# Softmax attention on one core: queries and keys of twelve pairs of heads transposed by TensorE and VectorE instead of by DMA, with other numbers in the planner

## The chip, the core and the metric

The kernel runs on one core of a Trainium2 chip. The metric is the device time of one execution in microseconds (us), as the median of several runs. A core has five engines that run side by side, each working through its own instructions in order: TensorE (PE, with its weight loads as PEld), VectorE (DVE), ScalarE (ACT), GpSimd (POOL) and SyncE (SP). SP does no arithmetic; here it issues nearly all DMA transfers. Transfers of all queues are carried out by the same 16 DMA engines.

## The reference

Attention over 8 batches and 8 heads, 512 positions, 64 dimensions, in float32:

```python
scale = 1.0 / np.sqrt(q.shape[-1])
scores = np.einsum('bhqd,bhkd->bhqk', q, k) * scale
scores = scores - scores.max(axis=-1, keepdims=True)
attn = np.exp(scores)
attn = attn / attn.sum(axis=-1, keepdims=True)
return np.einsum('bhqk,bhkd->bhqd', attn, v).astype(np.float32)
```

q, k and v are drawn from the standard normal distribution. The kernel takes no maximum off the scores.

## The kernel before

**Tiles.** The 64 heads are worked through as 32 pairs, g = 0 to 31. A pair's q, k and v are each one load of 128 partitions x 512 elements (256 KB). POOL casts them to float16: k and q into `qkp` (L343), v into one of 12 tiles `vp` (L335) that have a column of ones behind the 64 columns of v. For the scores, q and k have to stand with their dimension on the partitions, so `qkp` is transposed into `tqk`: partitions 0 to 63 hold the first head, 64 to 127 the second.

**Scores and exps.** A pair has 8 score blocks (c, h): chunk c of 128 keys of head h against all 512 queries. Two blocks make a group m, 128 groups of two in all but for the last two blocks, which stand alone. A group is two matmuls on TensorE (L396) into a PSUM tile `st` (128 x 1024 float32, 3 buffers), then one exp on ScalarE (L401) into a float16 tile `pt`. The exps of the first three groups are started by hand in `first_pair`. A few groups are "raised" instead: VectorE computes the exp with a polynomial, in one instruction that reads PSUM (`raise_`, L415) and six passes on SBUF (`pass_`, L428, L439 and four at L450).

**Values.** A unit is 128 queries of a head: four matmuls with 65 columns (L484), which add up the four chunks of `pt` against `vp`; the column of ones gives the softmax's sum. Seven units share a PSUM tile `o`, and VectorE normalises them together: a reciprocal (L462) and a multiply (L463) into a ring of results, from which SP stores each finished head (L471, 128 KB). The last head is computed chunk by chunk (`last_values`, L499 to L519).

**Transposes.** There are two ways. On TensorE: eight 128x128 transposes per pair (L370, `transposes`, in two halves of four, k first) into a PSUM tile `tp`, and one VectorE copy to `tqk` (L377, `copy`). The tiles `tp` and `o` take turns in two PSUM banks, `x0` and `x1`. By DMA: one DMA transpose per pair that SP issues (L353, `transpose_by_dma`) from `qkp` to `tqk`. The pairs listed in `Plan.BY_DMA` (6, 8, ... 28) go the second way, all others but pair 0 the first. Pair 0 has its own path.

**What sets the order.** Instructions are issued in a written order (`manual_schedule`). The class `Plan` computes it before the kernel is built: it steps through time, 5 ns at a time, with a fixed cost for each kind of work (`TRANSPOSE` 225 ns a half, `V_UNIT` 130, `SLOT` 216 for a score group, `COPY` 615, `PASSES` 690 to 1335 and so on), and decides at each point what TensorE (`step_pe`) and VectorE (`step_dve`) do next. TensorE takes the next score group if a PSUM tile and the transposed operands will be there, else a half transpose, else a unit of values. VectorE takes a raise first, then copies and normalisations as they become ready. It starts a polynomial pass only if the pass, its time multiplied by `MARGIN`, ends early enough for what is ready or soon will be (`LATE_NORM`, `LATE_COPY`). `for_dve` says which groups are raised: only while at most `AHEAD` passes are pending and not in the last `LAST_PAIRS` pairs. A raised exp counts as ready `SLACK` ns after its last pass. For pairs in `BY_DMA` the plan holds the operands to be there at time 0.

**The feed.** With every fourth group (`feed(g)`, at the first scores of pair g) the DMA transpose of pair g+2, the loads of pair g+5, the casts of q and k of pair g+3 and that of v of pair g+2 are issued. Loads have 6 buffers of each kind, `qkp` has 3, `tqk` has 5. SP works in order, so a load or store stands behind a DMA transpose that waits for its casts. Pairs in `HALVED` (only pair 20) have v loaded in two halves.

Of the kernel before, what the change touches and what calls it, by code (L numbers as in the profile page):

```python
# [9 lines left out]
FP16 = mybir.dt.float16  # L10
# [6 lines left out]
class Plan:  # L17
# [22 lines left out]
    STEP = 5  # L40
    FIRST_UNIT = 4

    BY_DMA = (6, 8, 10, 12, 14, 16, 18, 20, 22, 24, 26, 28)
    LATE_NORM, LATE_COPY, HURRY, SOON, BACKLOG = 600, 800, 1400, 220, 1600
    LAST_PAIRS, AHEAD, MARGIN, SLACK, MOST = 2, 1, 1.05, 800, 7

    def __init__(self, groups, pairs, first):
        self.groups, self.pairs = groups, pairs
# [4 lines left out]
        for m in range(first):  # L53
            self.act += self.EXP + self.EXP_FIXED
            self.exps[m] = self.act + self.EXP_DONE
            self.read.append(self.exps[m])
        self.tq = {0: 5800, **{g: 0 for g in self.BY_DMA}}
        self.next_t = 1
# [118 lines left out]
    def step_pe(self, t):  # L177
        if self.m == len(self.groups):
            self.values(t)
            return  # L180
        while self.part_t == 0 and self.next_t in self.BY_DMA:
            self.next_t += 1
# [62 lines left out]
def kernel(  # L245
# [7 lines left out]
    nc = tc.nc  # L253
    B, H, S, D = q.shape
    P = 128
# [18 lines left out]
    cpool = ctx.enter_context(tc.tile_pool(name="const", bufs=1))  # L274
    lpool = ctx.enter_context(tc.tile_pool(name="load", bufs=6))
    qpool = ctx.enter_context(tc.tile_pool(name="qk16", bufs=3))
    tpool = ctx.enter_context(tc.tile_pool(name="tqk", bufs=5))
    ppool = ctx.enter_context(tc.tile_pool(name="pt", bufs=30))
    dpool = ctx.enter_context(tc.tile_pool(name="pd", bufs=3))
    wpool = ctx.enter_context(tc.tile_pool(name="work", bufs=1))  # L280
# [3 lines left out]

    NV = 12

    HALVED = range(20, 21)
    NU = 56
    ring = cpool.tile([P, NU, D], FP32, name="ring")
    vps = [cpool.tile([P, 2, NI, D + 1], FP16, name=f"vp{n}") for n in range(NV)]  # L290
# [4 lines left out]
    qkp = {}  # L295
    tqk = {}
# [12 lines left out]
    def load_tile(g, name):  # L309
        t = lpool.tile(  # L310
            [P, 2, NI, D],
            FP32,
            tag=f"{name}32",
            name=f"{name}32_{g}",
            bufs=6,
        )
        raw.setdefault(g, {})[name] = t
        return t

    def load(g, names):  # L320
        if g >= NP:
            return
        for name in names:
            src = {"q": q, "k": k, "v": v}[name]
            t = load_tile(g, name)
            if name == "v" and g in HALVED:
                for h in range(2):
                    nc.sync.dma_start(out=t[:, h], in_=source(src, g)[:, h])
                continue
            nc.sync.dma_start(out=t[:, :, :, :], in_=source(src, g))  # L330

    def cast_v(g):
        if g >= NP:
            return
        nc.gpsimd.tensor_copy(out=vps[g % NV][:, :, :, 0:D], in_=raw[g]["v"][:, :, :, :])  # L335

    def cast_qk(g):
        if g >= NP:
            return
        t = qpool.tile([P, 2, NI, P], FP16, tag="qkp", name=f"qkp_{g}")  # L340
        for n, name in ((1, "k"), (0, "q")):
            eng = nc.vector if (g, name) == (1, "q") else nc.gpsimd
            eng.tensor_copy(  # L343
                out=t[:, n].rearrange("p i (h d) -> p h i d", h=2),
                in_=raw[g][name][:, :, :, :],
            )
        qkp[g] = t

    def transpose_by_dma(g):
        if g not in Plan.BY_DMA:  # L350
            return
        tqk[g] = tpool.tile([P, 2, S], FP16, tag="tqk", name=f"tqk_{g}")
        nc.sync.dma_start_transpose(  # L353
            out=tqk[g].rearrange("p n (i c) -> p (n i) c", c=P),
            in_=qkp[g].rearrange("p n i c -> p (n i c)"),
        )

    def feed(g):
        transpose_by_dma(g + 2)
        load(g + 5, "kqv")  # L360
        cast_qk(g + 3)
        cast_v(g + 2)
# [260 lines left out]
    with tc.manual_schedule():  # L623
        first_loads()
        load(1, "kq")
        load(0, "v")
        for g in range(2, 5):
            load(g, "kq")
            load(g - 1, "v")
        load(4, "v")  # L630
        make_identity(nc, ident)
        for n in range(NV):
            nc.vector.memset(vps[n][:, :, :, D : D + 1], 1.0)
        first_pair()
        cast_qk(1)
        cast_v(0)
        cast_qk(2)
        cast_v(1)
        feed(0)
        do = {  # L640
            "transposes": transposes,
            "scores": scores,
            "values": values,
            "feed": feed,
            "raise": raise_,
            "copy": lambda g, b: copy(g),
            "pass": pass_,
            "norm": lambda u, n, b: normalise(u, n),
        }
        for what, *args in Plan(groups, NP, 3).run():  # L650
            do[what](*args)
# [30 lines left out]
```

## Time and profile before

| | us |
|---|---|
| median of 3 runs | 129.43 (129.41 to 129.79) |
| the profiled execution | 129.41 |
| its span, first to last instruction | 127.6 |
| busy: ScalarE / TensorE / VectorE / POOL | 114.8 / 103.3 / 99.8 / 72.7 |
| exps on ScalarE (L401) | 119 instructions, 109.9 busy |
| score matmuls (L396) / value matmuls (L484) | 48.6 / 49.6 busy |
| copies of transposes (L377) | 18 instructions, 0.68 each |
| DMA transposes (L353) | 12, issue 1.27 each, landing 4.9 after issue |
| loads of q, k, v of 256 KB | landing 4.3 to 5.4 after issue |

A profile is of one execution. Its page gives the busy time of each engine, then the span in 40 equal slices, with a digit for the busy share in tenths; PEclk is the share of TensorE's clock that was granted, the DMA row the share of the 16 DMA engines that was in use. "Chain" is the line of work followed back from the last instruction to what released it. In the waits, "A <- B" means that engine and line A stood idle until B was done. In a timeline each row is a start, a duration, an engine with its line and operation, and how many instructions are merged; the idle time before it and what ended it are in brackets. Neighbouring rows of one engine can overlap, because an engine takes up the next instruction before the last has drained. In a table by windows each row is a stretch and its length, then the busy time of each engine with the number of instructions, the granted clock, the share of the DMA engines and GB/s.

### The profile page before, as it was taken

What the parts mean: (1) busy time and instruction counts of PE and PEld (TensorE: products, weight loads), DVE (VectorE), ACT (ScalarE), POOL (GpSimd) and SP (SyncE); (2) the same over time, 40 slices, a digit from 0 to 9 for tenths busy, and PEclk for the clock granted to TensorE, in tenths of its full rate; (3) what the DMA queues carried; (4) which work ended last, traced back from release to release, by engine and by line L of the source; (5) the groups of instructions that cost most, each with busy time, mean ns of one, the idle gap of its engine ahead of it and who ended that gap; (6) DMA issues with size and microseconds to landing.
All of it is one profiled execution on the core that took longest, in us unless ns stands there. A gap on an engine that the chain in (4) does not pass through costs nothing.

```text
span 127.6 us, 3742 instructions
## 1 busy us (share of the span) xinstructions
PE 103.3 (81%) x1461; PEld 62.3 (49%) x1461; DVE 99.8 (78%) x166; ACT 114.8 (90%) x126; POOL 72.7 (57%) x101
## 2 busy tenths in 40 slices
PE   7879799598693999859499399678997697999970
PEld 2545455275351665436344166246644374676550
DVE  1549999999795499979749599999999699636341
ACT  4789999999897799999959799999999999999970
POOL 2468989978474725564958099657757380700000
PEclk9999999999999599999967999999999999999998
DMA  4899999999998999999899799999999996943224
GB/s 127 273 362 382 380 382 380 231 374 226 358 319 266 383 302 371 215 337 343 114 376 360 226 374 365 377 205 385 359 372 266 311 341 163 380 138 123 85 100 149
DMA packets 48210, 36.95 MB, mean 290 GB/s; under 512 B 15296, under 2 KB 48192, under 8 KB 48192
## 3 DMA queue, kind: packets, MB, share of 16 engines
q1 hardware_dynamic: 47760, 36.38, 100.2%
q10 hardware_dynamic: 432, 0.33, 0.8%
q8 instruction: 11, 0.18, 0.5%
q14 instruction: 7, 0.06, 0.1%
HBM read 25.17 MB, written 8.39 MB: 263 GB/s over the span
## 4 chain that ended last, share of the span: by engine, by line
DMA 52%; PE 10%; DVE 9%; SPq 9%; POOL 8%; issue 5%; ACT 4%; POOLq 0%
DMA k<-in_k_dram 28%; DMA tqk<-qkp 13%; DMA v<-in_v_dram 9%; POOL qkp L343 6%; PE o L484 5%; PE st L396 4%; ACT pt L401 4%; SPq L353 3%; SPq L330 3%; DMA out_dram<-ring 3%; DVE ring L463 3%; SPq L471 2%; POOL vp L335 2%; DVE y L450 1%; DVE pt L450 1%
## 5 line engine op out<-in xcount | busy, mean ns | idle before, releaser
L401 ACT ACTIVATE pt<-st 128x1024 f16<-128x1024 f32 (+1 forms) x119 | 109.9, 1075 | 6.1 <-PE st L396 5.9
L396 PE MATMUL st<-tqk 64*128 64x512 f16 x248 | 48.6, 397 | 17.4 <-DMA tqk<-qkp 13.1
L484 PE MATMUL o<-vp,pt 128*128 128x65 f16 x1008 | 49.6, 197 | 1.5 <-ACT pt L401 0.7
L484 PEld LDWEIGHTS <-pt 128*128 128x128 f16 x1008 | 38.6, 99 | 23.9 <-issue 21.1
L343 POOL CAST qkp<-k 128x512 f16<-128x512 f32 x31 | 23.5, 759 | 33.1 <-DMA k<-in_k_dram 31.0
L335 POOL CAST vp<-v 128x512 f16<-128x512 f32 x32 | 26.5, 829 | 1.1 <-DMA v<-in_v_dram 1.0
L396 PEld LDWEIGHTS <-tqk 64*128 64x128 f16 x248 | 12.4, 93 | 27.8 <-DMA tqk<-qkp 14.5
L343 POOL CAST qkp<-q 128x512 f16<-128x512 f32 x30 | 23.9, 798 | 1.8 <-DMA q<-in_q_dram 1.6
L463 DVE TENSOR_TENSOR ring<-o,rc 128x448 f32<-128x448 f32 (+2 forms) x37 | 22.6, 612 | 1.3
L450 DVE SCALAR_TENSOR_TENSOR y<-y,m 128x1024 f32<-128x1024 f32 x14 | 18.9, 1350 | 0.0
L462 DVE RECIPROCAL rc<-o 128x7 f32<-128x7 f32 (+2 forms) x37 | 7.3, 198 | 13.0 <-PE o L484 12.9
L377 DVE COPY tqk<-tp 128x1024 f16<-128x1024 f16 x18 | 12.3, 683 | 3.0 <-PE tp L370 3.0
L370 PE MATMUL tp<-ident,qkp 128*128 128x128 f16 x152 | 12.6, 220 | 0.3 <-DVE rc L462 0.2
L370 PEld LDWEIGHTS <-qkp 128*128 128x128 f16 x152 | 8.6, 98 | 5.8 <-issue 4.2
L415 DVE TENSOR_SCALAR z<-st 128x1024 uint32<-128x1024 f32 x7 | 8.5, 1215 | 2.4 <-PE st L396 2.4
L450 DVE SCALAR_TENSOR_TENSOR y<-m 128x1024 f32<-128x1024 f32 x7 | 10.1, 1447 | 0.0
L450 DVE SCALAR_TENSOR_TENSOR pt<-y,e 128x1024 f16<-128x1024 f32 x7 | 9.3, 1324 | 0.0
L428 DVE TENSOR_SCALAR m<-z 128x1024 uint32<-128x1024 uint32 x7 | 6.6, 947 | 0.0
L439 DVE TENSOR_SCALAR e<-z 128x1024 uint32<-128x1024 uint32 x7 | 6.4, 916 | 0.0
L532 PE MATMUL st_0a<-const-bfloat16-1.0 128*128 128x512 bf16 (+1 forms) x11 | 3.2, 452 | 0.8 <-PEq L666 0.8
L548 ACT ACT_TABLE_LOAD x1 | 1.3, 1283 | 1.7 <-PEq L666 1.7
L532 PEld LDWEIGHTS <-const-bfloat16-1.0 128*128 128x128 bf16 x15 | 1.5, 119 | 2.4 <-issue 2.4
(43 smaller groups left out, 16.7 us busy)
## 6 DMA issues: line engine op xcount, KB each, us to landing
out_dram<-ring SPq DMA_DIRECT2D x63, 128.0 KB, 4.0
k<-in_k_dram SPq DMA_DIRECT2D x31, 256.0 KB, 4.3
q<-in_q_dram SPq DMA_DIRECT2D x31, 256.0 KB, 4.4
v<-in_v_dram SPq DMA_DIRECT2D x31, 256.0 KB, 5.4
q<-in_q_dram SPq DMA_DIRECT2D x2, 128.0 KB, 2.6
k<-in_k_dram ACTq DMA_DIRECT2D x2, 128.0 KB, 2.8
v<-in_v_dram SPq DMA_DIRECT2D x2, 128.0 KB, 4.0
tqk<-qkp SPq DMA_TRANSPOSE x12, 4.9
```

The source lines that it names most:

```text
L335: nc.gpsimd.tensor_copy(out=vps[g % NV][:, :, :, 0:D], in_=raw[g]["v"][:, :, :, :])
L343: eng.tensor_copy(out=t[:, n].rearrange("p i (h d) -> p h i d", h=2), in_=raw[g][name][:, :, :, :],)
L370: nc.tensor.transpose(tps[g][:, n, i, :], qkp[g][:, n, i, :], ident)
L377: nc.vector.tensor_copy(out=tqk[g][:, :, :], in_=tps.pop(g).rearrange("p n i c -> p n (i c)"))
L396: nc.tensor.matmul(st[:, x, :], kc, qc, start=True, stop=True)
L401: nc.scalar.activation(out=pt[:, 0:size, :], in_=st[:, 0:size, :], func=EXP, scale=scale)
L415: nc.vector.tensor_scalar(out=r["z"][:, :, :], in0=r["st"][:, :, :], scalar1=scale * 1.4426950408889634 * 2.0**23, scalar2=(127 + SHIFT) * ...
L428: nc.vector.tensor_scalar(out=r["m"][:, :, :], in0=r["z"][:, :, :], scalar1=0x007FFFFF, scalar2=0x3F800000, op0=AluOp.bitwise_and, op1=Alu ...
L450: nc.vector.scalar_tensor_tensor(out=r["pt"][:, :, :] if n == 3 else r["y"][:, :, :], in0=mant if n == 0 else r["y"][:, :, :], scalar=QUAR ...
L462: nc.vector.reciprocal(out=rc[:, 0:n], in_=o[:, x : x + n, D : D + 1])
L463: nc.vector.tensor_tensor(out=ring[:, u % NU : u % NU + n, :], in0=o[:, x : x + n, 0:D], in1=rc[:, 0:n].broadcast_to([P, n, D]), op=AluOp. ...
L484: nc.tensor.matmul(os[u // 7][:, u % 7, :], blocks[(g, c, h)][:, y * P : (y + 1) * P], vps[g % NV][:, h, c, :], start=(c == 0), stop=(c == ...
```

## The change

`BY_DMA` becomes empty, so that all pairs from 1 on are transposed on TensorE and copied by VectorE, and `transpose_by_dma` with its call is removed. The planner's numbers change: `LATE_NORM`, `LATE_COPY`, `SOON`, `LAST_PAIRS`, `AHEAD`, `MARGIN` and `SLACK`. `tqk` has four buffers instead of five. Five pairs (20 to 24) have v loaded in halves instead of one. Nothing else differs; behind the removed function the lines of the changed kernel have numbers that are lower by 10 (scores L386, exps L391, transposes L360, copies L367, values L474, normalisation L452 and L453).

```diff
-    BY_DMA = (6, 8, 10, 12, 14, 16, 18, 20, 22, 24, 26, 28)
-    LATE_NORM, LATE_COPY, HURRY, SOON, BACKLOG = 600, 800, 1400, 220, 1600
-    LAST_PAIRS, AHEAD, MARGIN, SLACK, MOST = 2, 1, 1.05, 800, 7
+    BY_DMA = ()
+    LATE_NORM, LATE_COPY, HURRY, SOON, BACKLOG = 400, 1400, 1400, 150, 1600
+    LAST_PAIRS, AHEAD, MARGIN, SLACK, MOST = 4, 0, 1.1, 1200, 7
...
-    tpool = ctx.enter_context(tc.tile_pool(name="tqk", bufs=5))
+    tpool = ctx.enter_context(tc.tile_pool(name="tqk", bufs=4))
...
-    HALVED = range(20, 21)
+    HALVED = range(20, 25)
...
-    def transpose_by_dma(g):
-        if g not in Plan.BY_DMA:
-            return
-        tqk[g] = tpool.tile([P, 2, S], FP16, tag="tqk", name=f"tqk_{g}")
-        nc.sync.dma_start_transpose(
-            out=tqk[g].rearrange("p n (i c) -> p (n i) c", c=P),
-            in_=qkp[g].rearrange("p n i c -> p (n i c)"),
-        )
-
     def feed(g):
-        transpose_by_dma(g + 2)
         load(g + 5, "kqv")
```

In the order that the planner writes, six groups are raised instead of seven.

## The prediction

> **What bounds the kernel now.** I read the page's head and clock first, then the chain of work that ended last, then the waits, and then ScalarE in order of time.
>
> ```profile
> span 127.6 us, 3742 instructions
> ...
> PE 103.3 (81%) x1461; PEld 62.3 (49%) x1461; DVE 99.8 (78%) x166; ACT 114.8 (90%) x126; POOL 72.7 (57%) x101
> ...
> PEclk9999999999999599999967999999999999999998
> DMA  4899999999998999999899799999999996943224
> ...
> DMA 52%; PE 10%; DVE 9%; SPq 9%; POOL 8%; issue 5%; ACT 4%; POOLq 0%
> ```
>
> ScalarE is the busiest engine. The DMA engines are all but full from the second slice to the 33rd of 40, and over half of the last chain is DMA. So ScalarE carries the most work, and the DMA queue decides how often it is starved. The waits (engine and line, what it waited for: us in all, times, longest) say through what:
>
> ```profile
> PE st L396 <- DMA tqk<-qkp: 13.1, 9, 2.1
> ...
> ACT pt L401 <- PE st L396: 5.9, 11, 1.0
> ...
> PE st L396 <- DVE tqk L377: 1.1, 2, 0.9
> ```
>
> TensorE stood 13.1 us before score matmuls whose operands a DMA transpose still had to deliver; ScalarE then stood 5.9 us before exps. ScalarE's timeline (start, duration, what, number merged, idle time before) shows where:
>
> ```profile
> 8.93 23.99 ACT L401 ACTIVATE pt<-st 128x1024 f16<-128x1024 f32 x26 [0.39 <-PE st L396]
> 33.49 6.59 ACT L401 ACTIVATE pt<-st 128x1024 f16<-128x1024 f32 x7 [0.56 <-PE st L396]
> 40.80 1.94 ACT L401 ACTIVATE pt<-st 128x1024 f16<-128x1024 f32 x2 [0.72 <-PE st L396]
> 43.23 1.02 ACT L401 ACTIVATE pt<-st 128x1024 f16<-128x1024 f32 x1 [0.50 <-PE st L396]
> 44.71 11.13 ACT L401 ACTIVATE pt<-st 128x1024 f16<-128x1024 f32 x12 [0.46 <-PE st L396]
> 56.15 7.44 ACT L401 ACTIVATE pt<-st 128x1024 f16<-128x1024 f32 x8 [0.31 <-PE st L396]
> 64.59 1.02 ACT L401 ACTIVATE pt<-st 128x1024 f16<-128x1024 f32 x1 [1.01 <-PE st L396]
> 66.12 1.02 ACT L401 ACTIVATE pt<-st 128x1024 f16<-128x1024 f32 x1 [0.50 <-PE st L396]
> 67.44 4.69 ACT L401 ACTIVATE pt<-st 128x1024 f16<-128x1024 f32 x5 [0.29 <-PE st L396]
> 73.04 35.31 ACT L401 ACTIVATE pt<-st 128x1024 f16<-128x1024 f32 x38 [0.91 <-PE st L396]
> 108.64 14.84 ACT L401 ACTIVATE pt<-st 128x1024 f16<-128x1024 f32 x17 [0.29 <-PE st L396]
> ```
>
> From 8.93 us to its last exp, which ends at 123.48, ScalarE has nothing but exps and these gaps. The first, 0.39, lies before any DMA transpose (the first is issued at 19.9). The ten others add up to 5.55 us. Six (0.56, 0.72, 0.31, 1.01, 0.91, 0.29; 3.80 in all) follow a TensorE wait for a transpose directly. Four (0.50, 0.46, 0.50, 0.29; 1.75) fall where the granted clock is 0.5, two stretches of about 3.4 us near 41 and 65 us. Each begins just after a transpose wait (1.98 us to 40.30, 2.09 us to 64.10), and TensorE was busy for only 1.44 of the 3.42 us from 38.08 on. So I put them down to the waits too.
>
> **The change, part by part.** *The transposes.* Twelve DMA transposes go; the instruction order of the changed program shows 62 half transposes (four 128x128 blocks each) on TensorE for 38, and VectorE copies for 31 pairs instead of 19. What one costs is read between starts, since these rows overlap. First two neighbours on TensorE, then two on VectorE:
>
> ```profile
> 110.65 0.62 PE L370 MATMUL tp<-ident,qkp 128*128 128x128 f16 x8
> 111.20 0.39 PE L396 MATMUL st<-tqk 64*128 64x512 f16 x2
> ```
>
> ```profile
> 13.71 0.68 DVE L377 COPY tqk<-tp 128x1024 f16<-128x1024 f16 x1
> 14.31 1.58 DVE L450 SCALAR_TENSOR_TENSOR y<-m 128x1024 f32<-128x1024 f32 x1
> ```
>
> Eight transposes take 0.55 us and one copy 0.60 us. TensorE gets 12 x 0.55 = 6.6 us more and loses the 13.1 us of waits, so it is less filled than its span is now. Does it keep up? A pair needs on TensorE four score groups (start to start about 0.32 each), 32 value matmuls in some four runs (a run of 16 takes 0.62, one of 8 takes 0.36, so 0.0325 a matmul and 0.10 a run: 1.44) and one transpose run of 0.55: 3.3 us. ScalarE needs 4 x 0.92 = 3.7 us, or 3.5 with its one group in 21 given to VectorE. It fits, with little over. And the stretch from 8.93 to 32.92 has run this way already: pairs 2 to 5 are transposed on TensorE one after the other, and ScalarE has 26 exps without a gap, at clock 1.00. In the last stretch, from 108.64, TensorE is busy 14.28 of 14.84 us and ScalarE still has no gap.
>
> VectorE gets 12 x 0.60 = 7.2 us and loses one of seven polynomial exps (six for seven in the order). One costs 1.21 + 0.95 + 0.92 + 1.45 + 2 x 1.35 + 1.32 = 8.55 us by its rows. VectorE is even: -1.3 us.
>
> *The exp that comes back.* ScalarE gets one group more: 0.92 us (25 steps in the 23.99 us stretch less its last 1.03 give 0.918, 37 in the 35.31 us stretch give 0.926). This is on the path: **+0.92**.
>
> *The gaps.* With the waits for the DMA gone, the ten go: **-5.55**. What is late next is ScalarE's own stream, and there is nothing to overtake it while TensorE holds 3.3 us a pair.
>
> *The queues.* SP loses 12 issues of 1.27 us, and with them the waits in front of them (6.4 us for casts of q and k, 3.9 for casts of v, 1.9 for a load), behind which loads and stores stood. The load of v in two halves, now for five pairs and not one, adds four issues at about 0.5 us (the issues of loads in the chain): SP gains on balance. Casts on POOL stay the same 3 a pair at about 0.61 us when undisturbed. The DMA engines:
>
> ```profile
> 10.00:15.00 5.00, 3.93 (x46) 2.12 (x44) 4.97 (x6) 5.00 (x6) 4.45 (x7) 1.00 1.10 385
> 50.00:55.00 5.00, 3.62 (x45) 2.04 (x44) 4.97 (x8) 5.00 (x7) 2.44 (x3) 1.00 1.15 257
> ```
>
> The last number is GB/s: with a transpose in it a stretch moves 257, without one 385, both at a full queue. Reads of 25.17 MB and writes of 8.39 MB take 33.56 / 0.385 = 87 us at the better rate, against some 115 us in which they are wanted. Loads stop deciding.
>
> *The planner's other numbers* (later due times, a raise only with no pass left, margin 1.1 for 1.05, no raise in the last four pairs) and four buffers for five have no row of their own. They act only by the order of copies and passes on VectorE. The twelve added copies can come late: 2 of 20 were waited for, 1.1 us of TensorE in all, so 12 more make 0.66 us at most if it all reaches ScalarE; it reached it with nothing (the 0.87 us wait at 14.44 lies in the gapless stretch). Ends 0 and 0.66, I take **+0.2**, near the row that shows nothing. Below nothing: if the 121 exps all step by 0.918 and not by the middle of 0.918 and 0.926, that saves 0.5 us, and the first gap of 0.39 can close too.
>
> **Sum.** Profiled execution 129.41 us, of it 127.6 span and 1.8 around it; the median of the runs is 129.43, the same. 129.41 - 5.55 + 0.92 + 0.2 = 124.98, so **125.0 us**. From ScalarE's last exp to the end of the span it is 4.1 us, and this tail (last values, normalise, store) is untouched.
>
> **A rule against it.** The row: eight transposes in 0.55 us, at clock 1.00 in 8.93 to 32.92. The Trainium skill's page "TensorE: Matmul & The Clock Gate", section "Part 4: PE-mode transpose", gives about 275 ns for one in a kernel and says that it doesn't count as busy time for the clock's gate. By that price 12 x 8 x 0.275 = 26.4 us would be added to TensorE, an estimate from the page, and the change would lose; the trace's rows decide against that price. The second half of the rule agrees with the two half-clock stretches here, which both have a transpose run in or just behind the idle time.
>
> **Rivals.**
> 1. *Half-clock stretches stay.* For: TensorE has some 0.2 us a pair to spare, so a stretch at 0.5 hurts. Against: none in the 24 us that already run like this, and what preceded both was a wait of 2 us. Price: two stretches as now cost 1.75 us: 126.7. At worst each loses half of 3.4 us, 3.4 in all: 128.4.
> 2. *Slower: copies behind polynomial passes.* VectorE runs in order. A copy that becomes ready as a pass begins waits up to 1.45 us; the next pair's scores stand behind it on TensorE, and all values behind these. With one score tile in hand (0.92) ScalarE loses 0.53 us. At half of the 24 pairs from 6 to 29 that is 6.4 us: 131.4; at all of them 137.7. It decides from (129.8 - 125.0) / 24 = 0.20 us a pair on. For: VectorE is busy for 33.17 of the 35.31 us from 73.04, so a copy seldom finds it idle, and one wait of 0.87 was seen. Against: 18 of 20 copies were on time.
> 3. *Nothing gained: loads set the pace anyway.* For: POOL waited 31.0 us for loads of k, the longest wait of all. Against: 87 us of transfers. If loads kept the mean of 290 GB/s the time would stay at 129.4. That the change doesn't do what it says belongs here; the order of instructions speaks against it.
>
> **How the numbers follow.** Forecast (124.0 to 126.0): 0.70. Half clock (126.0 to 128.4): 0.16. Late copies (over 129.8): 0.10. Loads (129.0 to 129.8): 0.04. The low end is 129.41 - 5.55 + 0.92 less 0.5 and 0.39, 123.9, put at 124.0; the high end takes in most of rival 1: 124.0 to 128.0 holds about 0.84. Faster by over 0.3% (0.39 us, about what a measurement here can tell from no change): 0.86; within: 0.04; slower: 0.10.
>
> **What would show it.** Right: no DMA transpose in the issues; ScalarE's waits for scores at or under 1 us in all; its exps one unbroken stretch from about 9 us to about 119; PEclk without a 5; mean DMA share well under full after 40 us. Wrong: TensorE waiting for copies of L367 over 5 us (rival 2), a 5 in PEclk (rival 1), POOL still waiting for loads and ScalarE with it (rival 3). TensorE filled without waits and ScalarE with gaps would break my 3.3 us a pair.

## The result, and the profile after

The changed kernel takes 123.85 us (median of four runs, 123.50 to 124.22), the kernel before 129.42 beside it. The ratio is 0.957, with a 95% interval of 0.953 to 0.960. (Here and below medians and ranges take in all runs; some executions fall in a slower state, and the ratios to the kernel before leave those out.) So it is faster by 5.6 us; 125.0 was forecast, and 123.85 lies 0.15 us under the low end of the range. The profiled execution took 123.50 us, of it 121.7 span. The page of the changed kernel, the lines that answer to those shown of before:

```profile
span 121.7 us, 3952 instructions
...
PE 109.3 (90%) x1557; PEld 68.5 (56%) x1557; DVE 97.0 (80%) x171; ACT 114.4 (94%) x127; POOL 74.0 (61%) x101
...
PEclk9999999999999999999999999999999999999999
DMA  3999999999999899899988989899999982131234
...
ACT 51%; PE 25%; issue 17%; DVE 4%; ACTq 0%
```

DMA has gone from the last chain, of which it had 52%; half of it is now ScalarE's own stream. The clock has no 5. TensorE has 6.0 us more work and is 90% busy. ScalarE in order of time:

```profile
8.22 109.42 ACT L391 ACTIVATE pt<-st 128x1024 f16<-128x1024 f32 x120
```

All 120 exps of L391 stand in one stretch of 109.42 us, in which the timeline prints no wait; the kernel before had eleven there, ten of them after its first DMA transpose. The waits of the changed kernel:

```profile
POOL qkp L343 <- DMA k<-in_k_dram: 14.7, 15, 1.9
...
PE st L386 <- ACT pt L391: 3.5, 12, 0.5
...
PE st L386 <- DVE tqk L367: 0.9, 1, 0.9
```

TensorE now waits for ScalarE (3.5 us in 12 waits: a score tile not yet read) and once for a copy, which reached ScalarE with nothing. POOL still waits 14.7 us for loads of k, half of what it waited before, and ScalarE doesn't pay for it. The kernel before:

```profile
POOL qkp L343 <- DMA k<-in_k_dram: 31.0, 21, 3.3
```

**Where the gain was made, by the ends of the exps.** In all profiles of this case two exps of 1024 columns in unbroken flow end 0.917 us apart. I call what an exp ends later than that ScalarE's loss, and add it up over a run from the starts and durations in the trace: 7.62 us before, 0.44 after, and all of the 0.44 lies before 9.4 us. This number serves for all experiments below; it is of one profiled execution each time.

### The profile page after: what moved, and what is told of

It reads as the page before. It is cut to its first block, busy times and chain, and to the rows that moved or that the text cites. A ratio compares the mean times of both kernels' runs of the same rounds, so it can differ in the third digit from the quotient of the medians.

```text
span 121.7 us, 3952 instructions
## 1 busy us (share of the span) xinstructions
PE 109.3 (90%) x1557; PEld 68.5 (56%) x1557; DVE 97.0 (80%) x171; ACT 114.4 (94%) x127; POOL 74.0 (61%) x101
## 4 chain that ended last, share of the span: by engine, by line
ACT 51%; PE 25%; issue 17%; DVE 4%; ACTq 0%
ACT pt L391 51%; PE st L386 8%; PE o L474 8%; PE tp L360 3%; PE st_0a L522 3%; DVE z L405 1%; PE st L565 1%; DVE tqk L365 1%; DVE tqk L367 1%; PE o_last L489 1%; DVE rc L452 0%; PE tp_qb L560 0%; DVE qt L602 0%; DVE obl L502 0%; PE st_0a L565 0%
## 5 line engine op out<-in xcount | busy, mean ns | idle before, releaser
L391 ACT ACTIVATE pt<-st 128x1024 f16<-128x1024 f32 (+1 forms) x120 | 109.4, 1327 | 0.1
L386 PE MATMUL st<-tqk 64*128 64x512 f16 x248 | 48.5, 384 | 5.9 <-ACT pt L391 3.5
L474 PE MATMUL o<-vp,pt 128*128 128x65 f16 x1008 | 48.6, 195 | 1.5 <-ACT pt L391 1.3
L474 PEld LDWEIGHTS <-pt 128*128 128x128 f16 x1008 | 37.5, 98 | 21.0 <-issue 16.7
L343 POOL CAST qkp<-k 128x512 f16<-128x512 f32 x31 | 26.5, 854 | 24.3 <-DMA k<-in_k_dram 14.7
L453 DVE TENSOR_TENSOR ring<-o,rc 128x448 f32<-128x448 f32 (+2 forms) x37 | 22.6, 612 | 1.3
L386 PEld LDWEIGHTS <-tqk 64*128 64x128 f16 x248 | 14.1, 93 | 16.8 <-issue 6.9
L343 POOL CAST qkp<-q 128x512 f16<-128x512 f32 x30 | 22.1, 738 | 1.1 <-DMA q<-in_q_dram 0.6
L367 DVE COPY tqk<-tp 128x1024 f16<-128x1024 f16 x30 | 20.5, 685 | 2.5 <-PE tp L360 2.2
L360 PE MATMUL tp<-ident,qkp 128*128 128x128 f16 x248 | 19.9, 220 | 0.0
L360 PEld LDWEIGHTS <-qkp 128*128 128x128 f16 x248 | 14.0, 98 | 7.3 <-issue 5.2
L452 DVE RECIPROCAL rc<-o 128x7 f32<-128x7 f32 (+2 forms) x37 | 7.4, 201 | 11.9 <-PE o L474 11.4
L440 DVE SCALAR_TENSOR_TENSOR y<-y,m 128x1024 f32<-128x1024 f32 x12 | 15.8, 1313 | 0.0
L440 DVE SCALAR_TENSOR_TENSOR y<-m 128x1024 f32<-128x1024 f32 x6 | 8.0, 1330 | 0.0
L440 DVE SCALAR_TENSOR_TENSOR pt<-y,e 128x1024 f16<-128x1024 f32 x6 | 7.4, 1231 | 0.0
L418 DVE TENSOR_SCALAR m<-z 128x1024 uint32<-128x1024 uint32 x6 | 4.6, 772 | 0.1
```

Source lines behind the costliest of these rows:

```text
L343: eng.tensor_copy(out=t[:, n].rearrange("p i (h d) -> p h i d", h=2), in_=raw[g][name][:, :, :, :],)
L360: nc.tensor.transpose(tps[g][:, n, i, :], qkp[g][:, n, i, :], ident)
L367: nc.vector.tensor_copy(out=tqk[g][:, :, :], in_=tps.pop(g).rearrange("p n i c -> p n (i c)"))
L386: nc.tensor.matmul(st[:, x, :], kc, qc, start=True, stop=True)
L391: nc.scalar.activation(out=pt[:, 0:size, :], in_=st[:, 0:size, :], func=EXP, scale=scale)
L440: nc.vector.scalar_tensor_tensor(out=r["pt"][:, :, :] if n == 3 else r["y"][:, :, :], in0=mant if n == 0 else r["y"][:, :, :], scalar=QUAR ...
```

## Experiments

Theory 1: the DMA transposes alone made the loss, because the DMA queue has no room for them. Rivals: the planner's numbers carry the gain; a transpose is late by its own latency; the half clock is a cause by itself; copies behind polynomial passes.

**e1, only the list emptied.** The planner's old numbers stay.

```diff
-    BY_DMA = (6, 8, 10, 12, 14, 16, 18, 20, 22, 24, 26, 28)
+    BY_DMA = ()
```

> The kernel before with the list of pairs for DMA transposes emptied; the planner's old numbers, five tqk buffers and one halved load stay. Theory 1 (the DMA transposes alone made the loss, the planner's numbers hardly matter): the DMA waits and nearly all of ScalarE's gaps go; seven groups are raised, so ScalarE has one group (0.92 us) less than the changed kernel, but the last raise comes late (group 107) and can lengthen the tail: 123.0 to 125.5 us. Rival (the planner's new numbers carry the gain): 127.5 us or more, with TensorE waiting for copies.

Measured 123.48 us (before 129.25 in the same runs, ratio 0.954, 0.949 to 0.960). By the order that the planner writes here, the values of pair 26's second head come behind those of the last head, and that head is never stored: one of 64 stores, and the normalisation of its last unit, are left out. (The changed kernel's order stores all heads; so far the new numbers are needed.) ScalarE's loss is 0.52 us. In time the list alone gives the whole gain; the rival falls.

**e2, the new numbers with the old list**, and five halved loads.

```diff
-    LATE_NORM, LATE_COPY, HURRY, SOON, BACKLOG = 600, 800, 1400, 220, 1600
-    LAST_PAIRS, AHEAD, MARGIN, SLACK, MOST = 2, 1, 1.05, 800, 7
+    LATE_NORM, LATE_COPY, HURRY, SOON, BACKLOG = 400, 1400, 1400, 150, 1600
+    LAST_PAIRS, AHEAD, MARGIN, SLACK, MOST = 4, 0, 1.1, 1200, 7
...
-    HALVED = range(20, 21)
+    HALVED = range(20, 25)
```

> The kernel before with the planner's new numbers and five halved loads, the twelve DMA transposes kept (and five tqk buffers). Theory 1: 129.4 within 0.8 us, TensorE still waits some 13 us for DMA transposes. Rival (the numbers carry the gain): under 126.5 us.

Measured 132.69 us, ratio 1.025 (1.019 to 1.031): slower than before, which neither theory had. The gain isn't in the numbers. **e10** has the halved loads alone:

```diff
-    HALVED = range(20, 21)
+    HALVED = range(20, 25)
```

> The kernel before with one of the smaller edits alone: v loaded in halves for pairs 20 to 24. It tells what made e2_list_new_numbers slower than before by 3 us. If the four more DMA issues did it, 131 us or more; if the planner's numbers did it, 129.3 within 0.8.

Measured 132.52 us in four runs from 129.96 to 133.48, ratio 1.014 (1.001 to 1.027). That is too wide to tell: the halved loads cost between nothing and 2.7%. How the 2.5% of e2 divide between them and the numbers stays open.

**e3, room made in the queue.** The kernel before, all twelve DMA transposes kept, without 56 of the 64 stores of L471 (the output is left incomplete).

```diff
             g, h, u0 = heads.pop(0)
+            if g < 28:
+                continue
             nc.sync.dma_start(
```

> The kernel before, which stores only the heads of the last four pairs: 56 of 64 stores, 7.3 MB, are left out. Theory 1 in its form 'the DMA queue has no room': 7.3 MB at 385 GB/s is 19 us of queue time, about what I estimate for the twelve transposes (a 5 us stretch moved 257 GB/s instead of 385, so 1.7 us each, 20 in all); loads and transposes come in time, TensorE waits under 4 us for DMA transposes, PEclk without a 5, 123.0 to 125.5 us. Rival (a transpose is late because it is issued late and takes 4.9 us, whatever else is in the queue): TensorE still waits over 9 us, 128.0 to 129.4 us.

Measured 122.81 us, ratio 0.949 (0.945 to 0.954), just under the theory's range. From the waits of this kernel:

```profile
POOL qkp L343 <- DMA k<-in_k_dram: 1.7, 2, 1.4
...
ACT pt L401 <- PE st L396: 0.3, 1, 0.3
PE st L396 <- DMA tqk<-qkp: 0.3, 1, 0.3
```

The wait for transposes falls from 13.1 us to 0.3, POOL's for loads of k from 31.0 to 1.7. ScalarE's loss is 0.71 us. Twelve DMA transposes cost next to nothing when the stores are away, and they still land 4.7 us after their issue, for 4.9 before: so it isn't their own latency, they were issued too late. (With the stores went SP's time to issue them and its waits in front of them, 9.2 us for results before; this run doesn't part that from the room in the DMA engines.) Against the expectation the clock still has one half stretch:

```profile
PEclk9999999999999999999999999769999999999999
```

It begins near 77.3 us with no wait for a DMA in front of it: in the 3.4 us before, TensorE had only stood three times for ScalarE or VectorE (0.43, 0.49 and 0.33 us).

**e4, the traffic without the dependency.** The changed kernel with the twelve transfers put back, into a tile that nobody reads.

```diff
+    def transpose_by_dma(g):
+        if g not in range(6, 29, 2):
+            return
+        spare = tpool.tile([P, 2, S], FP16, tag="spare", name=f"spare_{g}", bufs=2)
+        nc.sync.dma_start_transpose(
+            out=spare.rearrange("p n (i c) -> p (n i) c", c=P),
+            in_=qkp[g].rearrange("p n i c -> p (n i c)"),
+        )
+
     def feed(g):
+        transpose_by_dma(g + 2)
         load(g + 5, "kqv")
```

> The changed kernel with the same twelve DMA transposes put back in the same places, but into a spare tile that nobody reads; TensorE and VectorE transpose all pairs as in the changed kernel. Theory 'no room in the queue': loads of k come late again, POOL waits 25 us or more for them, and TensorE's transposes and ScalarE behind them lose part of it: 125.5 to 129 us. Rival 'only the dependency of the scores on the late transfer': 123.9 us within 0.5, since nobody waits for the transfers.

Measured 128.87 us, ratio to before 0.997 (0.993 to 1.001): the gain is all but gone, though no instruction waits for these transfers. What comes late instead is in the waits:

```profile
POOL qkp L343 <- DMA k<-in_k_dram: 22.7, 17, 4.1
...
PE tp L370 <- POOL qkp L343: 4.5, 12, 1.4
...
ACT pt L401 <- PE st L396: 2.7, 6, 0.9
```

Loads of k land late (POOL waits 22.7 us for them, a little under the 25 expected), the casts come behind them, and TensorE's transposes wait for casts. ScalarE's loss is 4.50 us, 4.06 more than in the changed kernel. So the transfers do harm without anybody waiting for them, by what they delay.

**e5, six of the twelve**, with the new numbers and halved loads of e2.

```diff
-    BY_DMA = (6, 8, 10, 12, 14, 16, 18, 20, 22, 24, 26, 28)
+    BY_DMA = (6, 10, 14, 18, 22, 26)
```

> The kernel before with the planner's new numbers and five halved loads (the kernel of e2_list_new_numbers), but with DMA transposes for six pairs only (6, 10, 14, 18, 22, 26). Theory 'no room in the queue': six transposes at an estimated 1.7 us are 10 us of queue time on top of 87 us for loads and stores, which leaves room in some 113 us, so the loss nearly vanishes and doesn't halve; seven raised groups take 0.92 off ScalarE and a late last raise puts about 1.0 on the tail: 123.3 to 125.5 us, TensorE waits under 4 us for DMA transposes. Rival (each DMA transpose costs its own fixed wait): half way between 132.7 and 123.9, 127.5 to 129 us.

Measured 129.99 us, in runs from 128.15 to 131.70, ratio 0.991 (0.986 to 0.996). TensorE still waits 5.2 us for DMA transposes, where under 4 was expected. My reckoning of the room falls: six transposes don't fit in for nothing. Against the kernel before they leave nearly the whole time, but that kernel has the old numbers. Among the three kernels with the new ones the ratio to before is 0.957 without DMA transposes, 0.991 with six and 1.025 with twelve (e2), so each six cost about the same 3.4%. Half way is what the rival forecast; its cause, a fixed wait that each transpose brings with it, doesn't fit e3 and e4. Where my reckoning went wrong can be seen in the page's line for the queue, before and changed:

```profile
q1 hardware_dynamic: 47760, 36.38, 100.2%
```

```profile
q1 hardware_dynamic: 35152, 33.24, 83.7%
```

The last column is the time of all packets as a share of the span. Packets overlap: the stretch from 10 to 15 us that the prediction shows, filled with loads alone, has a share of 1.10. Share times span, here called queue time, is therefore no time on the clock, but kernels can be compared by it. Beside it stands the time that SP spends on issuing DMA transfers, added up from the trace (all in us):

| kernel | DMA transposes | queue time | SP issuing | ScalarE's loss |
|---|---|---|---|---|
| before | 12 | 1.002 x 127.6 = 127.9 | 95.0 | 7.62 |
| e4 | 12, unread | 0.991 x 126.2 = 125.1 | 99.3 | 4.50 |
| e5 | 6 | 0.905 x 126.4 = 114.4 | 86.1 | 4.80 |
| e3, no stores | 12 | 0.861 x 121.2 = 104.4 | 70.8 | 0.71 |
| changed | 0 | 0.837 x 121.7 = 101.9 | 74.5 | 0.44 |
| e1 | 0 | 0.830 x 121.9 = 101.2 | 74.8 | 0.52 |

In this measure loads and stores take 101.9 us; the prediction's 87 us, at its share of 1.10, would be 96. A transpose takes (127.9 - 101.9) / 12 = 2.2 us; the 1.7 of the expectations, at the share of 1.15 in its row, would be 1.9. The kernels with over 110 us lose 4.5 us and more, those under 105 lose under 0.8. It is no straight line over all of them: e5 and e4 lose about the same, but in e4 nobody waits for the transposes.

**What these runs don't part** is the room in the DMA engines and the time of SP, which issues nearly all transfers in order. SP's column divides the kernels just as the queue time does, and e3 and e4 move both. For the engines: from 36 to 106 us their share is 1.16 before and 0.89 in the changed kernel, and before at least four of SP's transfers are at every moment issued and not yet landed. For SP: in the same stretch it is issuing for 88% of the time before and in e4, 68% in the changed kernel; and a load of k takes no longer from issue to landing before (median 4.3 us) than in the changed kernel (4.9), so it comes late because it is issued late. SP's standing for casts in front of the transposes isn't the loss by itself: before it stands 10.3 us there, in e3, which loses next to nothing, 24.3:

```profile
SPq L353 <- POOL qkp L343: 13.0, 7, 2.4
SPq L353 <- POOL vp L335: 11.3, 5, 3.4
```

So the runs show that the transposes among the loads and stores make the loads late. Which of the two is short, the engines or SP, stays open.

**e6 and e11, the half clock.** e6 puts dummy matmuls in front of the first scores of all twelve DMA pairs, e11 only in front of pairs 10 and 16, whose waits preceded the two half-clock stretches (`range(5)` and a test for these two).

```diff
+        if grp[0][0] in Plan.BY_DMA and grp[0][1:] == (0, 0):
+            for n in range(6):
+                busy(st[:, 0], S)
         for x, (g, c, h) in enumerate(grp):
```

> The kernel before, with six dummy matmuls of 512 columns (some 1.3 us) on TensorE ahead of the first scores of each of the twelve DMA pairs, written into the score tile that the scores then overwrite. Theory (the half-clock stretches come from TensorE's idle time before late transposes): no 5 in PEclk, the four gaps of ScalarE inside those stretches (2.2 us with what follows each) go, the other gaps stay: 126.5 to 128.3 us. Rival (the clock falls for another reason, or the dummies delay TensorE as much as they save): 128.8 us or more.

> The kernel before with five dummy matmuls of 512 columns (some 1.1 us) ahead of the first scores of pairs 10 and 16 alone, where TensorE stood 1.98 and 2.09 us before the two half-clock stretches. Theory (those waits bring on the half clock): no 5 in PEclk near 41 and 65 us and up to 2.2 us less: 127.0 to 128.5 us. Rival (TensorE's idle time over a wider stretch does it, or the waits lie elsewhere from run to run): a 5 is there still, 129 us or more.

e6: 133.70 us, ratio 1.028 (1.020 to 1.035): the dummies cost more than they could save, and the profile, of the slowest of its four runs, has a half stretch still. It decides nothing. e11: 129.60 us, ratio 1.002 (0.997 to 1.007). The page of e11:

```profile
PEclk9999999999999999599999999999999999999997
```

The stretches near 41 and 65 us are gone; a new one stands at 51 us, two pairs on, behind a wait of 1.74 us for another transpose. The loss, 6.75 us, is 0.9 lower than before, the time is not. Neither theory holds as it was put. In this one profile filling a wait took away its own half stretch; but a wait for a DMA isn't needed for one (e3; e4 has one from 75.0 us on, behind a wait of 1.35 us for a cast), and an idle TensorE isn't enough: in the kernel before it was busy for only 1.34 of the 3.40 us from 70.40 on, and the clock stayed at 1.00. What sets it is open.

**e7, copies held up** (the prediction's second rival), in the changed kernel:

```diff
-    LATE_NORM, LATE_COPY, HURRY, SOON, BACKLOG = 400, 1400, 1400, 150, 1600
+    LATE_NORM, LATE_COPY, HURRY, SOON, BACKLOG = 4000, 4000, 1400, 150, 1600
```

> The changed kernel with both due-time numbers at 4000, so that the planner starts a polynomial pass whatever copy or normalisation is about to be ready: the prediction's second rival, made on purpose. Seven groups are raised and the last of them ends late, which by the order puts some 2.5 us of value work behind the last exp. Rival 2 as priced (0.53 us of ScalarE a pair at half the pairs and more): gaps of ScalarE of 5 us or more in all, 128 us or more. Theory (the written order already puts other TensorE work in front of late copies, so ScalarE is not starved): gaps under 1.5 us, 124.5 to 126.3 us.

Measured 126.01 us, ratio 0.970 (0.964 to 0.977). ScalarE from its first gap on:

```profile
9.52 107.42 ACT L391 ACTIVATE pt<-st 128x1024 f16<-128x1024 f32 x118 [0.54 <-PE st L386]
```

The loss is 0.64 us: the stream holds. TensorE stood before scores for a copy once, 1.2 us (0.9 in the changed kernel), so in the order that the planner writes the delay hardly reaches it; a kernel in which many copies come late to TensorE was not run. The price appears at the end. The last exp ends at 116.94 and the span at 124.7, a tail of 7.8 us for 4.1 in the changed kernel, with a run of 88 value matmuls, 22 units, on TensorE from 115.40 us to 118.63.

**e8, e9 and e12, seven raised groups.** e8 is the changed kernel with:

```diff
-    LATE_NORM, LATE_COPY, HURRY, SOON, BACKLOG = 400, 1400, 1400, 150, 1600
-    LAST_PAIRS, AHEAD, MARGIN, SLACK, MOST = 4, 0, 1.1, 1200, 7
+    LATE_NORM, LATE_COPY, HURRY, SOON, BACKLOG = 400, 1000, 1400, 150, 1600
+    LAST_PAIRS, AHEAD, MARGIN, SLACK, MOST = 4, 0, 1.0, 1200, 7
```

> The changed kernel with LATE_COPY 1000 and MARGIN 1.0, which gives seven raised groups instead of six. Theory (ScalarE's unbroken stream sets the time, each group 0.917 us): 0.92 us less for ScalarE, some 0.5 us more of tail: 123.4 us, 0.2 to 0.9 us under the changed kernel. Rival (VectorE or TensorE is now as close): no gain or slower, 123.9 to 125 us, with gaps in ScalarE's stream.

It took 123.34 us, ratio 0.952 (0.948 to 0.956). e9 is the changed kernel and e12 the kernel of e8, side by side on one chip:

> The changed kernel itself once more, beside e12_seven_again on the same chip, as the base of that comparison: 123.9 us within 0.4; the granted clock at full all through; ScalarE loses under 0.7 us against a stream of exps that end every 0.917 us.

> The kernel of e8_seven_raised once more, on the same chip as the changed kernel. ScalarE has one group fewer, 0.92 us; the last profile lost 1.0 us in gaps where the changed kernel lost 0.4, and its tail is longer: 0.2 to 0.8 us faster than e9_changed_again. If VectorE's seventh group gives nothing on balance: within 0.2 us.

e9: 123.55 us (ratio to before 0.957, 0.952 to 0.963), a loss of 0.57 us; its clock has a 5, against the expectation, but only in the last two slices, where its tail is 0.7 us longer than in the first profile of this kernel. e12: 123.25 us (0.956, 0.950 to 0.961), a loss of 1.27 us. The group saved on ScalarE (0.92) comes back as loss (0.70 more than e9). 0.3 us is within what can be told apart, so I claim no better version.

## Why the prediction was right in kind and too small

Term by term, from the two profiled executions, 129.41 and 123.50 us (exp ends from the trace; the medians, 129.42 and 123.85, differ by 0.34 less):

| term of the sum | forecast | measured |
|---|---|---|
| ScalarE's gaps | -5.55 | -7.62 + 0.44 = -7.18 |
| one group more on ScalarE | +0.92 | +0.92 |
| copies that come late | +0.2 | 0 |
| first full exp ends at 7.13, not 6.71 | not named | +0.42 |
| behind the last exp, and around the span | 0 | -0.07 |
| sum | -4.43 | -5.91 |

**The mechanism held.** The DMA transposes starved ScalarE, by their own lateness and by that of the loads behind them; without them its stream is unbroken, TensorE carries 6.0 us more (6.6 forecast) and VectorE 97.0 us instead of 99.8. e1 and e4 show both directions. Of rival 2, e7 finds a price in the tail and none in ScalarE's gaps. Rival 3 was closer than I put it: 102 us of queue time for my 96 (87 at a share of 1.10), and the DMA share from 36 to 106 us is 0.89, not "well under full".

**The step that failed is "With the waits for the DMA gone, the ten go: -5.55".** I added up the idle times that the timeline prints in brackets. An exp in flow ends 0.917 us after the one before it, but the first after a gap takes 1.02 from its start to its end, as rows show that the prediction quoted: the exp that starts at 66.12 after 0.50 of idle time ends at 67.14, the one before it at 64.59 + 1.02 = 65.61, so 1.53 us apart, a loss of 0.61 and not of 0.50. Ten gaps are worth 6.61 us so, 1.06 more than printed. Five stalls too short to be printed (at 25.5, 35.4, 45.7, 81.4 and 100.9 us) hold another 0.52, and the start changes by 0.05: 7.18 in all. So this term of the sum was too small by 1.63 us. The low end was built from other things (a spread of the exps' step, the first gap) and so missed this. The step itself was misread too: 0.918 and 0.926 have such short stalls in them (0.06 us in the first of the two stretches, 0.37 in the second); by ends, without them, it is 0.917 in both.

**The +0.42 at the start is scatter, not the change.** In the thirteen other profiled executions, with the old list and with the new one, the first full exp ends between 7.03 and 7.26 us; the profile of before, at 6.71, was early.

**"With a transpose in it a stretch moves 257" was no price of a transpose.** The changed kernel has stretches as slow with none in it, loads and stores together:

```profile
46.00:52.00 6.00, 5.78 (x96) 3.96 (x94) 5.13 (x9) 6.00 (x8) 3.73 (x4) 1.00 0.90 242
```

385 GB/s was the rate of loads alone, before the first store, which is issued at 18.5 us. That error didn't move the forecast, which took the loads as no limit in the changed kernel, and ScalarE indeed lost nothing to them; it went into what was expected of e5.

**The half-clock stretches** were 2.18 us of the 7.62 by this ledger. No kernel without DMA transposes (changed, e1, e7, e8, e9, e12) shows one ahead of its last two slices. That they come from the transpose waits alone, as the prediction put it, is not shown: e3 and e4 speak against it, e11 half for it.

**The rule of the Trainium skill** (page "TensorE: Matmul & The Clock Gate", section "Part 4: PE-mode transpose") that a transpose takes about 275 ns in a kernel doesn't hold as a price per transpose here: the trace prints 220 ns for one, but they overlap: a run of eight takes 0.55 us, and with 96 more of them TensorE's busy time rose by 6.0 us, some 63 ns each. That by the same section they don't count as activity for the clock did no harm: with 248 of them among 1557 matmuls the clock stayed full in the changed kernel's profile.

## What to carry to other kernels

Price the gaps of the engine that sets the time by the distance between ends, not by the idle time that the profile prints: here the first exp after a gap cost 0.10 us beside the idle time, and short stalls weren't printed at all. Before you give a transfer to a DMA queue that others use, look at how full it and its issuing engine are: here twelve transposes cost 0.7 us or less where 56 stores had been taken out, and about 3.4% (4.4 us) for each six where they hadn't (e5, e2). A transfer that nobody waits for can cost most of what a waited-for one costs, because what it delays are the loads behind it.

## What the runs showed of the hardware that was not expected

An exp's printed duration grows in an unbroken stream, from 1.02 us after a gap to as much as 1.65 in the changed kernel, while the ends stay 0.917 apart: the mean of L391 is 1.33 us there against 1.08 of L401 before, and it is the faster kernel. Four stretches of the changed kernel with stores among the loads move 242 to 318 GB/s at a queue share of 0.87 to 1.00; with loads nearly alone, from 10 to 20 us, it is 382 at 1.09.
